# Last gate and mixed low parts shared with GpSimd, second GLA decay two flushes later, gates from slot 0, first pair's keys by halves, three loads by ACT

## Chip, core and metric

The kernel runs on one core of one Trainium2 chip. The metric is the device time of one execution in microseconds (us), median of several runs. Five queues work side by side: TensorE (PE, with its weight loads PEld), VectorE (DVE), ScalarE (ACT), GpSimd (POOL) and SyncE (SP, which only issues transfers). ACT and POOL issue transfers too.

## What is computed

Two layers of a hybrid encoder over 1040 positions (16 meta tokens and 1024 frames) of width 1024, in float32. Cut to what matters here:

```python
xn = rms_norm(h, attn_norm[i])
gq, gk, gv, gr, glr, fq, fk, fv, ff = split(xn @ w_in[i])
log_a = log_sigmoid(glr @ w_alpha_up[i] + b_alpha[i]) / 16
o_gla = rms_norm(gla_chunk_causal(gq / 8, gk, gv, log_a), gla_norm[i]) * silu(gr)   # 4 heads
o_fox = rms_norm(forgetting_attention(fq, fk, fv, log_sigmoid(ff + b_forget[i])), fox_norm[i])  # 8 heads
h = h + concat(o_gla, o_fox) @ w_out[i]
h = h + conv_ffn(rms_norm(h, ffn_norm[i]), w_up[i], conv_w[i], conv_b[i], w_down[i])
# after both layers: rms_norm(h, final_norm)[16:]
```

GLA is linear attention with a decay: per chunk of 64 frames a state S = decay * S + k^T v is kept and read by the queries. FoX is softmax attention with a bias that sums the log of a forget gate.

## The kernel before

Activations lie transposed: eight tiles of 128 features by 1040 positions. A float32 matmul is made of three matmuls in a reduced-width format, `mm3` (L261 to L263): each operand is split into a high part `hi`, a rounded copy made by ACT, and a low part `lo` = x - hi, a subtraction, mostly on DVE. The rounded product hi*hi and the two cross products are added up in PSUM. The helper `split` (L374) does it for activations, at lines L377 (copy by ACT) and L378 (subtraction by DVE); `weights` (L219, L228, L230) does it for weight tiles that SP loads.

A layer has an attention stage and an FFN stage; the change touches the first alone. The attention stage runs in this order.

1. **Head** (`head`). The input tiles are normalised and split in three column chunks (`norm_split`, L341 on ACT and L342 on DVE), and the low-rank and forget projections (L424, L428) and the first GLA projections are made of them. In layer 0 the input comes from memory: `load(0)` in `run` issues eight transfers for the first chunk (L1849), of which those of tiles 1 and 3 go by ACT's queue and six by SP's. Twelve warm-up matmuls (L943) run before.
2. **GLA pair 0 and pair 1.** Each pair has two heads. `gla_products` makes keys, values and queries; when the last key chunk is evacuated, `ev_k` appends `gla_decay` to `self.later`, a list that `flush` empties: it runs what it holds at the end of the next unit of matmuls. `gla_decay` makes z (L507, three PSUM tiles of tag S), a log-sigmoid, a scan over the positions (L510), two more passes and the final product into the keys (L521). `gla_steps` makes the states (L562), reads them (o, L574, which uses three tiles of tag S and one of tag av), normalises each read (L587 to L596) and transposes the result (L603). Between these steps it calls `fill`, which runs the next projection's matmuls in the PE's free time: pair 1's products fill pair 0's steps, and the FoX products of head pair 0 fill pair 1's.
3. **FoX**, `fox`, with four head pairs. A hand-written list of 72 steps, 18 a pair, goes through query tiles; each step is a slot n. In a slot, scores S (L718, L719) go to DVE (L721, bias added, running minimum) and ACT (L733, exp, P); two slots later P is transposed by PE (L754, L747), split (L377, L378) into PT, and in the slot after that used by `av` (L780). `plan(p)` gives the filling work that is spread over the slots from `starts[p]` on: for p = 0 to 2 the products of the next head pair (`fox_products`) and one gate (`gr_products`, silu(gr) times the GLA output), for p = 3 the last gate, for p = 4 the first four tiles of the output projection. `starts` is 4, 22, 40, 58, 62 and 80. At a turn from one plan to the next the old work is drained first.
4. **The turn to the output projection**, slot 62. `plan(4)` splits the mixed activations of the last column chunk (256 columns, seven of the eight tiles, `land[k]` into `mix[k]`, order KORD = 4, 5, 0, 1, 2, 3, 6), asks POOL to load the residual into the tiles just split (L1056), and queues units of matmuls; the other two chunks are split when their first unit begins. Of the last gate, `gr_products(3)`, the result goes straight into `land[3]` (`dst`).

`fox_products` writes keys in two forms, per head: kA holds the high part and kL the low part, each in both halves of the partitions. `ev_k` casts the chunk to kA[0] (L639, ACT), subtracts into kL[0] (L640, POOL), and after the last chunk SP copies halves about, three transfers for kA and three for kL (L644); the third of each overwrites a half that the first two read.

The framework that the kernel is written in orders the instructions of every queue when the program is built, by the order of the code and its own estimates of durations; `high_priority` and the due slots steer it. So an instruction can stand earlier or later in its queue than in the code. Once built, the order in each queue is fixed. In the FFN stage PE's order is that of the code.

Of the kernel before, what the change touches and what calls it, by code (L numbers as in the profile page):

```python
# [170 lines left out]
class Kern:  # L171
# [199 lines left out]
            self.rsqrt_mean(r, ps[:, :n], y0[:, :n], a[:, :n], nm.pop("pin", False))  # L371
        return r

    def split(self, hi, lo, src, scale=None):  # L374
        nc = self.nc
        if scale is None:
            nc.scalar.copy(hi, src)  # L377
            nc.vector.tensor_tensor(out=lo, in0=src, in1=hi.bitcast(F32), op=ALU.subtract)  # L378
        else:
            nc.scalar.mul(hi, src, scale)  # L380
            nc.vector.scalar_tensor_tensor(out=lo, in0=src, scalar=scale, in1=hi.bitcast(F32),
                                           op0=ALU.mult, op1=ALU.subtract)
# [61 lines left out]
    def gla_products(self, lyr, p, gp, pp, nm, g):  # L444
        nc = self.nc
        s = self.slots
        rs = lambda c0, n: self.norm_scale(nm, pp, c0, n)
        g["gk"] = gk = s.get(F32, "gk")
        g["gq"] = gq = s.get(F32, "gq")
        g["gv"] = [s.get(F32, "gv", (128, 8, 128)) for _ in range(2)]  # L450
        g["gvm"] = gvm = gp.tile([64, 2, 128], F32, tag="gvm", name="gvm", bufs=2)
        nc.gpsimd.memset(gvm[:], 0.0)
        if p == 0:
            self.kdm = gp.tile([64, 128], F32, tag="kdm", name="kdm", bufs=1)
            nc.gpsimd.memset(self.kdm[:], 0.0)

        def ev_k(ps, c0, n):
            nc.vector.tensor_tensor(out=gk[:, c0:c0 + n], in0=ps, in1=rs(c0, n), op=ALU.mult)
            if c0 + n == T:
                self.later.append(lambda: self.gla_decay(lyr, p, gp, pp, g))  # L460

        def ev_q(ps, c0, n):
            nc.vector.scalar_tensor_tensor(out=gq[:, c0:c0 + n], in0=ps, scalar=0.125, in1=rs(c0, n),
                                           op0=ALU.mult, op1=ALU.mult)

        def ev_v(hh):
            def ev(ps, c0, n):
                vt = gp.tile([128, 400], F32, tag="vt", name="vt", bufs=3)
                nc.vector.tensor_tensor(out=vt[:, :n], in0=ps, in1=rs(c0, n), op=ALU.mult)
                self.later.append(lambda: self.to_natural(pp, vt, c0, n, self.gv_store(g["gv"][hh], gvm, hh)))  # L470
            return ev
        W = lambda m: self.wm[lyr, m]
        return [(W(M_GK + p), ev_k), (W(M_GV + 2 * p), ev_v(0)), (W(M_GV + 2 * p + 1), ev_v(1)), (W(M_GQ + p), ev_q)]
# [139 lines left out]
    def fox_products(self, lyr, p, work, sp, pp, nm, q, w=None):  # L613
# [21 lines left out]
        def ev_k(ps, c0, n):  # L635
            cs = slice(c0, c0 + n)
            t = sp.tile([128, 400 if self.vt_bufs == 3 else 348], F32, tag="vt", name="kt", bufs=self.vt_bufs)[:, :n]
            nc.vector.tensor_tensor(out=t, in0=ps, in1=rs(c0, n), op=ALU.mult)
            nc.scalar.copy(kA[0][:, cs], t)  # L639
            nc.gpsimd.tensor_tensor(out=kL[0][:, cs], in0=t, in1=kA[0][:, cs].bitcast(F32), op=ALU.subtract)  # L640
            if c0 + n == T:
                for k in (kA, kL):
                    for to, x, own in ((k[1], hi, hi), (k[1], lo, hi), (k[0], hi, lo)):
                        nc.sync.dma_start(to[x, :T].bitcast(F32), k[0][own, :T].bitcast(F32))  # L644
# [25 lines left out]
    def gr_products(self, lyr, h, work, ap, pp, nm, dst=None):  # L670
        nc = self.nc

        def ev(ps, c0, n):
# [8 lines left out]
            nc.scalar.activation(e, e, AF.Exp, scale=-1.0)  # L682
            nc.scalar.activation(y, e, AF.Ln, bias=self.ones[:, 0:1])
            nc.scalar.activation(y, y, AF.Exp, scale=-1.0)
            nc.vector.tensor_tensor(out=og, in0=x, in1=og, op=ALU.mult)
            nc.vector.scalar_tensor_tensor(out=e, in0=e, scalar=1.0, in1=y, op0=ALU.add, op1=ALU.mult)
            nc.vector.scalar_tensor_tensor(out=y, in0=e, scalar=-2.0, in1=y, op0=ALU.add, op1=ALU.mult)
            to = og if dst is None else dst[:, c0:c0 + n]
# [140 lines left out]
    def fox(self, lyr, ap, pp, qs, plan, mix3):  # L829
# [5 lines left out]
        steps = [(p, g, e, ti) for p in range(4) for g in range(5) for e in range(2)  # L835
                 for ti in reversed(range(len(groups[g])))]
        first = [steps.index((p, 0, 0, 1)) for p in range(4)]
        starts = [f + 4 for f in first] + [first[3] + 8, len(steps) + 8]
        cbs, state, due = {}, {}, {}
        work, p_next = plan(-1), 0  # L840

# [7 lines left out]
        for n in range(len(steps) + 8):  # L849
# [30 lines left out]
                    self.fox_mask(cbs[p][e], i - 1)  # L880
                self.fox_schedule(lyr, at, n, p, e, ti, i, tiles, Ps, st, qs[p], ap, pp, mix3)
            parts = [c for c in "12" if (n, "av" + c) in due or (n, "T" + c) in due]
            work.run(fill_us / (1 + len(parts)))
            run(n, "store")
            run(n, "fold")
            for c in parts:
                run(n, "av" + c)
                run(n, "T" + c)
                work.run(fill_us / (1 + len(parts)))
        work.drain()  # L890
        self.slots.put(*cbs[3])
        self.fox_free(qs[3])
# [52 lines left out]
    def attention(self, lyr, nm, hsrc, chunks, feed):  # L945
        tc, nc, s = self.tc, self.nc, self.slots
        self.ch, self.ctiles = CH_HEAD[lyr], CT_HEAD[lyr]
        with tc.tile_pool(name=f"aps{lyr}", bufs=2, space=PSUM, reuse_waits="tile") as pp2, \
# [64 lines left out]
            with tc.tile_pool(name=f"att{lyr}", bufs=2, reuse_waits="tile") as ap, \  # L1013
# [5 lines left out]
                def plan(p):  # L1019
# [15 lines left out]
                    elif p == 4:  # L1035
# [14 lines left out]

                        def split(j):
                            c0, n = chunks[j]
                            for k in KORD:
                                self.split(mix[k][0][:, c0:c0 + n], mix[k][1][:, c0:c0 + n], land[k][:, c0:c0 + n])
                            for m in range(NSPLIT):
                                nc.gpsimd.dma_start(hT[m][:, c0:c0 + n], hsrc[m][:, c0:c0 + n])  # L1056
                        split(2)
# [778 lines left out]
    def run(self):  # L1836
# [3 lines left out]
        def feed(src):  # L1840
# [4 lines left out]
            def load(j):  # L1845
                c0, n = ch[j]
                for k in range(KD):
                    eng = nc.scalar if j == 0 and k in (1, 3) else nc.sync
                    eng.dma_start(land[k][:, c0:c0 + n], self.hT0[k, :, c0:c0 + n])  # L1849
            w = self.narrow_weights(src)  # L1850
            return {"w": w, "load": load,
# [98 lines left out]
```

## Time and profile before

| what | us |
|---|---|
| median of the 3 runs before (lowest to highest) | 2472.36 (2470.87 to 2472.37) |
| the profiled execution: its own time | 2473.53 |
| its span, first to last instruction of the program | 2471.5 |
| outside the span in that execution | 2.0 |
| layer 0: head, GLA, FoX, then FFN | about 0 to 44, 171, 500, then 1240 |
| layer 1: the same | about 1240 to 1286, 1399, 1729, then the end |

A row of the timeline gives start, duration, queue, line, operation, output<-inputs and shape, then in brackets the idle time of the engine before it and who ended that. A row of the waits gives who waited for whom: total us, times, the longest. A row of the windows gives the stretch, its length, then busy time and instructions of each queue, the granted TensorE clock, the busy share of the transfer engines and GB/s. A row on a line or a tile gives shortest, median and longest duration in ns.

### The profile page before, as it was taken

Reading aid. Unit: us, or ns where it says so; the run is one execution under the profiler, and the core shown is the slowest. Engines: PE = TensorE matmul, PEld = TensorE weight load, DVE = VectorE, ACT = ScalarE, POOL = GpSimd, SP = SyncE. Lnnn points to the kernel's source line nnn. Section 1 sums busy time; section 2 is a strip of 40 time slices with the busy share of each in tenths; the row PEclk is TensorE's granted clock in tenths of the full one; section 3 lists DMA queues with packets and bytes.
Section 4 is the critical chain, followed back from the end, with each engine's and each line's share of the span. In section 5 each row is a group of like instructions: output and inputs, shape, how many; then the busy total and the mean of one; then the engine's idle time right before and its main releaser. Section 6 shows DMA issues by size and latency. Waiting matters only on the chain.

```text
span 2471.5 us, 47309 instructions
## 1 busy us (share of the span) xinstructions
PE 2440.1 (99%) x18286; PEld 2358.4 (95%) x18286; DVE 1873.4 (76%) x3769; ACT 1318.1 (53%) x2857; POOL 384.9 (16%) x565
## 2 busy tenths in 40 slices
PE   9999999999999999999999999999999999999998
PEld 8999999999999999999999999999999999998887
DVE  8665776869988888855866666777699888887667
ACT  7345766646555555642543456666465555556433
POOL 2023433210000000100220234331100000001002
PEclk9999999999999999999999999999999999999999
DMA  3222134443322224764312222243433212247722
GB/s 131 74 84 76 43 95 130 126 124 104 119 76 83 83 73 144 185 161 140 118 47 74 80 78 71 71 142 108 146 84 116 91 65 90 82 151 184 210 71 88
DMA packets 121680, 260.39 MB, mean 105 GB/s; under 512 B 15248, under 2 KB 37008, under 8 KB 121456
## 3 DMA queue, kind: packets, MB, share of 16 engines
q1 hardware_dynamic: 97008, 182.18, 23.8%
q0 software_dynamic: 22288, 72.81, 10.5%
q8 instruction: 143, 2.34, 0.4%
q10 hardware_dynamic: 2160, 2.38, 0.3%
q14 instruction: 81, 0.66, 0.1%
HBM read 176.74 MB, written 67.80 MB: 99 GB/s over the span
## 4 chain that ended last, share of the span: by engine, by line
PE 48%; issue 31%; DVE 13%; ACT 4%; DMA 2%; POOL 1%; SPq 0%; DVEq 0%; POOLq 0%; ACTq 0%
PE mm L261 7%; PE mm L263 7%; PE mm L262 7%; PE down L262 4%; PE down L261 4%; PE down L263 4%; PE av L780 3%; PE tr L754 2%; PE S L718 1%; DVE x L1188 1%; DVE S L721 1%; PE S L719 1%; ACT P L733 1%; DVE lo L1163 1%; DMA raw<-in_wm_dram 1%
## 5 line engine op out<-in xcount | busy, mean ns | idle before, releaser
L262 PE MATMUL up<-x,lo 128*128 128x260 f32 x2240 | 632.0, 282 | 0.9 <-DVE lo L1163 0.8
L261 PE MATMUL up<-x,hi 128*128 128x260 f32 x2240 | 632.0, 282 | 0.1
L263 PE MATMUL up<-x,hi 128*128 128x260 f32 x2240 | 632.0, 282 | 0.0
L262 PEld LDWEIGHTS up<-x,lo 128*128 128x128 f32 x2240 | 421.9, 188 | 1.4 <-DVE lo L1163 1.3
L261 PEld LDWEIGHTS up<-x,hi 128*128 128x128 f32 x2240 | 421.9, 188 | 0.4 <-ACT hi L1162 0.3
L263 PEld LDWEIGHTS up<-x,hi 128*128 128x128 f32 x2240 | 422.1, 188 | 0.0
L1162 ACT CAST hi<-raw 128x512 fp32r<-128x512 f32 (+1 forms) x490 | 266.3, 553 | 208.5 <-PE up L263 89.6
L261 PE MATMUL mm<-xh,hi 128*128 128x348 f32 (+6 forms) x1056 | 359.8, 341 | 0.0
L1163 DVE TENSOR_TENSOR lo<-raw,hi 128x512 fp32r<-128x512 f32 (+1 forms) x490 | 286.8, 600 | 81.3 <-ACT hi L1162 80.8
L263 PE MATMUL mm<-xl,hi 128*128 128x348 f32 (+6 forms) x1056 | 339.7, 322 | 0.0
L262 PE MATMUL mm<-xh,lo 128*128 128x348 f32 (+6 forms) x1056 | 338.7, 321 | 0.0
L261 PEld LDWEIGHTS mm<-xh,hi 128*128 128x128 f32 x1056 | 199.5, 189 | 2.3 <-issue 1.4
L262 PEld LDWEIGHTS mm<-xh,lo 128*128 128x128 f32 x1056 | 199.4, 189 | 0.3
L263 PEld LDWEIGHTS mm<-xl,hi 128*128 128x128 f32 x1056 | 198.6, 188 | 0.1
L1144 DVE TENSOR_TENSOR raw<-raw,raw 128x512 f32<-128x512 f32 (+1 forms) x230 | 146.8, 648 | 28.9 <-DMA raw<-in_wd_dram 26.3
L733 ACT ACTIVATE P<-S,m 116x460 f32<-116x460 f32 (+2 forms) x224 | 124.9, 562 | 77.1 <-DVE m L721 74.3
L228 ACT CAST hi<-raw 128x512 fp32r<-128x512 f32 (+2 forms) x152 | 87.4, 576 | 140.5 <-PE mm L263 59.6
L262 PE MATMUL down<-x,lo 128*128 128x260 f32 (+1 forms) x504 | 161.2, 320 | 0.6 <-DVE lo L1163 0.6
L263 PE MATMUL down<-x,hi 128*128 128x260 f32 (+1 forms) x504 | 161.2, 320 | 0.0
L261 PE MATMUL down<-x,hi 128*128 128x260 f32 (+1 forms) x504 | 161.1, 320 | 0.0
L378 DVE TENSOR_TENSOR PT<-tr,PT 116x464 fp32r<-116x464 f32 (+3 forms) x240 | 123.1, 515 | 48.9 <-ACT PT L377 47.2
L1424 POOL DMA_DIRECT2D actd<-cv x44 | 23.6, 535 | 734.5 <-DVE cv L1423 734.5
(313 smaller groups left out, 5957.8 us busy)
## 6 DMA issues: line engine op xcount, KB each, us to landing
raw<-in_wm_dram SPq DMA_DIRECT2D x326, 256.0 KB, 3.0
raw<-in_wd_dram SPq DMA_DIRECT2D x48, 256.0 KB, 4.4
actd<-cv POOLq DMA_DIRECT2D x22, 520.0 KB, 3.0
actd<-cv POOLq DMA_DIRECT2D x22, 512.0 KB, 2.9
cb<-cd SPq DMA_DIRECT2D x16, 520.0 KB, 3.9
kA<-kA SPq DMA_DIRECT2D x24, 260.0 KB, 4.0
kL<-kL SPq DMA_DIRECT2D x24, 260.0 KB, 4.7
st<-actd SPq DMA_DIRECT2D x24, 260.0 KB, 3.7
```

Source lines behind the costliest of these rows:

```text
L228: nc.scalar.copy(hi[:, :n, :], raw[:, :n, :])
L261: nc.tensor.matmul(ps, wh, xh[:, c0:c0 + n], start=first, stop=False, skip_group_check=more)
L262: nc.tensor.matmul(ps, wl, xh[:, c0:c0 + n], start=False, stop=False, skip_group_check=more)
L263: nc.tensor.matmul(ps, wh, xl[:, c0:c0 + n], start=False, stop=last, skip_group_check=more)
L378: nc.vector.tensor_tensor(out=lo, in0=src, in1=hi.bitcast(F32), op=ALU.subtract)
L718: nc.tensor.matmul(S[:rows, :n], q["qA"][e][:, qs], q["kA"][e][:, c0:k1], start=True, stop=False)
L733: nc.scalar.activation(P[:rows, :n], S[:rows, :n], AF.Exp, scale=-1.0, bias=m[:rows, nch - 1:nch], accum_out=(den if nch == 1 else d3[:row ...
L754: nc.tensor.transpose(tr[:w, 3 - j, :rows], P[:rows, o:o + w], id_)
L780: nc.tensor.matmul(av[:, a:b], w.rearrange("p a b -> p (a b)"), x, start=(t == ts[0] and part == 0 and i == 0), stop=(t == last and i == 1))
L1144: nc.vector.tensor_tensor(out=q[out][:, :nk, :], in0=q[a][:, :nk, :], in1=q[b][:, :nk, :], op=op)
L1162: nc.scalar.copy(hi[:, :nk, :], src[:, :nk, :])
L1163: nc.vector.tensor_tensor(out=lo[:, :nk, :], in0=src[:, :nk, :], in1=hi[:, :nk, :].bitcast(F32), op=ALU.subtract)
```

## The change

Seven edits:

- `split` can be told which engine subtracts. In `plan(4)` the subtractions of tiles 5, 1 and 3 (every second one of KORD) go to POOL, in all three chunks; the copies stay with ACT.
- In the last gate alone, the product gx * gog (L685) goes to POOL.
- Pair 1's decay is appended twice more before it runs, so two flushes later. Pair 0's stays.
- `starts[0]` is 0 instead of 4: the filling work of the first head pair is spread over slots 0 to 21.
- In slot 62 the filling work is run at the slot's end, after the slot's store, fold, av and transposes, instead of in two or three shares between them.
- For head pair 0, ACT and POOL write each head's keys from the half where they lie, two instructions of 64 partitions instead of one of 128, and SP copies each half once to the other: four transfers instead of six.
- Of the eight first loads, tile 5's goes by ACT's queue as well.

```diff
-    def split(self, hi, lo, src, scale=None):
+    def split(self, hi, lo, src, scale=None, eng=None):
...
-            nc.vector.tensor_tensor(out=lo, in0=src, in1=hi.bitcast(F32), op=ALU.subtract)
+            (eng or nc.vector).tensor_tensor(out=lo, in0=src, in1=hi.bitcast(F32), op=ALU.subtract)
...
-                self.later.append(lambda: self.gla_decay(lyr, p, gp, pp, g))
+                decay = lambda: self.gla_decay(lyr, p, gp, pp, g)
+                wait = lambda f: lambda: self.later.append(f)
+                self.later.append(wait(wait(decay)) if p else decay)
...
+            if p == 0:
+                for e, own in enumerate((lo, hi)):
+                    nc.scalar.copy(kA[e][own, cs], t[own])
+                    nc.gpsimd.tensor_tensor(out=kL[e][own, cs], in0=t[own], in1=kA[e][own, cs].bitcast(F32),
+                                            op=ALU.subtract)
+                if c0 + n == T:
+                    for k in (kA, kL):
+                        for e, own, oth in ((0, lo, hi), (1, hi, lo)):
+                            nc.sync.dma_start(k[e][oth, :T].bitcast(F32), k[e][own, :T].bitcast(F32))
+                return
...
-            nc.vector.tensor_tensor(out=og, in0=x, in1=og, op=ALU.mult)
+            (nc.vector if dst is None else nc.gpsimd).tensor_tensor(out=og, in0=x, in1=og, op=ALU.mult)
...
-        starts = [f + 4 for f in first] + [first[3] + 8, len(steps) + 8]
+        starts = [0] + [f + 4 for f in first[1:]] + [first[3] + 8, len(steps) + 8]
...
-            work.run(fill_us / (1 + len(parts)))
+            turn = n == starts[4]
+            if not turn:
+                work.run(fill_us / (1 + len(parts)))
...
-                work.run(fill_us / (1 + len(parts)))
+                if not turn:
+                    work.run(fill_us / (1 + len(parts)))
+            if turn:
+                work.run(fill_us)
...
-                            for k in KORD:
-                                self.split(mix[k][0][:, c0:c0 + n], mix[k][1][:, c0:c0 + n], land[k][:, c0:c0 + n])
+                            for i, k in enumerate(KORD):
+                                self.split(mix[k][0][:, c0:c0 + n], mix[k][1][:, c0:c0 + n], land[k][:, c0:c0 + n],
+                                           eng=nc.gpsimd if i % 2 else None)
...
-                    eng = nc.scalar if j == 0 and k in (1, 3) else nc.sync
+                    eng = nc.scalar if j == 0 and k in (1, 3, 5) else nc.sync
```

## The prediction

> **What bounds the kernel now.** I began with the page: its first two lines of numbers, then the waits of PE, then the windows around the places that the change touches.
>
> ```profile
> span 2471.5 us, 47309 instructions
> PE 2440.1 (99%) x18286; PEld 2358.4 (95%) x18286; DVE 1873.4 (76%) x3769; ACT 1318.1 (53%) x2857; POOL 384.9 (16%) x565
> ```
>
> PE is busy 2440.1 of 2471.5 us, so all idle time of PE is 31.4 us, and the change removes no matmul. It can win only from those 31.4 us, and from matmuls that run at a low clock. Which of them it can reach, the waits of PE tell (total, times, longest):
>
> ```profile
> PE mm L263 <- DVE ml L378: 3.5, 2, 1.8
> PE tr L754 <- DVE PT L378: 3.1, 4, 1.2
> PE S L718 <- ACT P L733: 1.9, 4, 0.6
> ...
> PE av L780 <- DVE PT L378: 1.4, 5, 0.4
> PE tr L603 <- DVE on L596: 1.4, 1, 1.4
> PE z L507 <- DVE on L596: 1.4, 1, 1.4
> PE mm L428 <- DVE xl L342: 1.3, 1, 1.3
> ...
> PE av L780 <- ACT PT L377: 0.7, 2, 0.3
> ...
> PE o L574 <- DVE B L390: 0.4, 1, 0.4
> ```
>
> Nearly all of them come once a layer, at four places: the turn to the output projection (ml, PT), the start of FoX (P), the second decay (on, B) and, in layer 0 only, the head (xl). The two turns are the worst:
>
> ```profile
> 445.00:465.00 20.00, 16.61 (x128) 15.77 (x127) 19.87 (x58) 17.28 (x49) 6.22 (x12) 1.00 0.37 105
> 1673.00:1693.00 20.00, 16.88 (x129) 15.56 (x127) 19.87 (x59) 17.63 (x50) 6.03 (x12) 1.00 0.34 98
> ```
>
> In 20 us PE is idle 3.4 and 3.1, while DVE is busy 19.87: there DVE is the bound, and POOL, at 6, is free.
>
> **The turn.** These are the last two steps of DVE ahead of PE's first wait in layer 0, then PE's two long waits and what stands between them:
>
> ```profile
> 450.90 0.51 DVE L685 TENSOR_TENSOR gog<-gx,gog 128x344 f32<-128x344 f32 x1
> 451.33 1.09 DVE L378 TENSOR_TENSOR ml<-h,mh 128x256 fp32r<-128x256 f32 x3
> ...
> 451.80 0.39 PE L263 MATMUL mm<-ml,hi 128*128 128x256 f32 x1 [1.76 <-DVE ml L378]
> ...
> 453.09 0.79 PE L780 MATMUL av<-PT,V 116*128 116x232 f32 x6
> 453.71 0.49 PE L754 MATMUL tr<-ident,P 116*116 116x116 f32 x3
> ...
> 457.62 0.61 PE L754 MATMUL tr<-ident,P 116*116 116x116 f32 x4 [1.22 <-DVE PT L378]
> ```
>
> The first fill of the slot needs, 1.76 us before 451.80, a low part that DVE begins at 451.33. Three edits act here. The gate product (0.51) leaves DVE ahead of that low part. Three of the seven subtractions leave DVE: 3 x 0.42 = 1.3 us for this chunk (the row of three takes 1.09, since they overlap a little; 0.42 is one alone). And the slot's av and transposes, 453.09 to 454.20, so 1.1 us of PE work that came behind the stall, now come before the fill.
>
> On POOL such a subtraction is dearer; the same shape stands there in other places, as do two instructions that show a conflict:
>
> ```profile
> L355 POOL TENSOR_TENSOR r<-r,sq 128x256 f32<-128x256 f32 x14 | 10.6, 760 | 7.1 <-ACT sq L354 6.9
> ...
> 153.62 0.92 POOL L640 TENSOR_TENSOR kL<-kt,kA 128x344 fp32r<-128x344 f32 x1 [1.69 <-issue]
> ...
> 153.66 0.90 DVE L315 TENSOR_TENSOR oa<-oa,ovv 128x4 f32<-128x4 f32 x1
> ...
> 154.86 0.16 DVE L315 TENSOR_TENSOR oa<-oa,ovv 128x4 f32<-128x4 f32 x1
> ```
>
> 0.76 us on POOL for 0.42 on DVE. And a DVE operation on 4 columns, 0.16 us by itself, took 0.90 when it began 0.04 us behind a POOL subtraction, and ended 0.02 behind it: it was held until POOL was done. The remaining DVE subtractions read two SBUF operands like it. The worst price per chunk is therefore 3 x 0.76 = 2.3 held less 1.3 saved = 1.0 us lost on DVE; the best is 1.3 won. I take half of the loss, 0.5, since ACT's copies come in between and DVE has PSUM-sourced work for some of that time.
>
> The Trainium skill's page "SBUF — State Buffer", section "SBUF: two separate sides", speaks against this edit: DVE operations with two SBUF inputs and GpSimd share a port pair as an exclusive lock, held for a whole instruction, and the loser blocks. The row of 0.90 agrees. By that rule alone the sharing costs the 1.0 and not the 0.5.
>
> Per turn: the first stall, 1.76, loses 1.1 (PE work ahead) and 0.5 (gate product) and gets back 0.5 (held DVE), a gain of 1.1. The second, 1.22 and 1.07, is a PT subtraction late on the same full DVE queue; by then DVE has lost a second 0.5 or three 0.42s, and I take half, 0.6. Of the small ones behind (0.4 and 0.2) I take 0.2. That is 1.9 a turn, **3.8** for both layers; ends: 6.5 won (all idle time of both windows), 2.0 lost.
>
> **The start of FoX.** The four waits for P and two for PT are 1.9 + 0.7 = 2.6 us, about 183 to 191 in layer 0 and 1410 to 1418 in layer 1. The keys come late:
>
> ```profile
> 159.67 1.17 SPq L644 DMA_DIRECT2D kA<-kA  x2
> 160.88 2.28 SPq L644 DMA_DIRECT2D kL<-kL  x2
> ...
> 166.93 0.46 SPq L644 DMA_DIRECT2D kL<-kL  x1
> ...
> kL<-kL SPq DMA_DIRECT2D x24, 260.0 KB, 4.7
> ```
>
> SP cannot issue the third copy of kL until the first two have been read and landed, and this last issue, at 166.93, lands 4.7 us later by the median, about 171.6; scores that need kL cannot run before. By halves nothing is overwritten: the four transfers go out at about 160 to 162.5 and the last lands near 167, some 4.5 us earlier. The edit adds, a layer, three ACT casts and three POOL subtractions:
>
> ```profile
> L639 ACT CAST kA<-kt x24: 478/482/486, 153.0 to 1616.9; 128x348 fp32r<-128x348 f32 x16, 128x344 fp32r<-128x344 f32 x8
> ...
> L640 POOL TENSOR_TENSOR kL<-kt,kA x24: 917/928/953, 153.6 to 1618.3; 128x348 fp32r<-128x348 f32 x16, 128x344 fp32r<-128x344 f32 x8
> ```
>
> The length along the columns is the same, so 0.48 and 0.93 each. ACT and POOL have idle time at 150 to 165 (POOL's wait of 1.69 above); only the last chunk's pair, 1.4 us, delays the transfers, which is in the 162.5. If that cover were gone, the price is 1.4 us a layer out of 4.5.
>
> `starts[0]` = 0 spreads the same fill over 22 slots instead of 18, so each gets 18/22 of it, but slots 0 to 3 now have some in their own order. PE stays fed while the first P are made. What is late next are the slots from 4 on, with 18% less fill each; the PT waits in the first pairs are 0.1 to 0.2 us, and I put 0.7 us on that and the added ACT and POOL work, for both layers. I take **2.2** of 2.6 as won; ends: 2.6 won, 0.8 lost.
>
> **The decay.** Pair 1's decay runs between pair 0's reads and their norms:
>
> ```profile
> 92.11 2.32 DVE L510 TENSOR_TENSOR_SCAN A<-reset,B 128x1040 f32<-128x1040 bf16 x1
> ...
> 97.11 0.23 PE L603 MATMUL tr<-ident,on 16*128 16x16 f32 x1 [1.38 <-DVE on L596]
> 97.12 1.22 DVE L521 TENSOR_TENSOR gk<-gk,B 128x1040 f32<-128x1040 f32 x1
> ...
> 115.06 0.71 PE L603 MATMUL tr<-ident,on 128*128 128x128 f32 x5
> ...
> 128.58 1.04 PE L536 MATMUL tr<-ident,gk 128*128 128x128 f32 x8
> ```
>
> The scan alone holds DVE 2.32 us while PE waits 1.38 for a norm, and the z tiles hold PSUM that the reads want (0.4, the wait of o for B). In layer 1 PE stands at z itself, 1.4 us, since its PSUM tile is still being read by a norm. Two flushes are two units of matmuls, some 7 us: z moves behind the first norms. All of it is 1.4 + 1.4 + 0.4 = 3.2 us. What is late next: the third z takes the PSUM tile that the last norm reads, and the decay's 8 us of DVE meet the last norms, whose transposes stand at 115.06. The decay ends with its product into the keys, 98.3 before; two units and the wait for the third z bring it to about 114, and the keys are transposed at 128.58, so that end keeps a cover of 14 us. I take **2.0** won; ends: 3.2 won, 1.4 lost (one such wait more).
>
> **The head.** ACT's queue is free until 3.6:
>
> ```profile
> 1.19 3.24 SPq L1849 DMA_DIRECT2D hin<-in_hT_dram  x6
> 3.62 0.71 ACT L244 CAST both<-raw 128x256 fp32r<-128x256 f32 x2 [1.59 <-DMA raw<-in_wr_dram]
> ...
> 8.74 0.52 ACT L341 ACTIVATE xh<-hin,gain 128x272 fp32r<-128x272 f32 x1 [1.08 <-DMA hin<-in_hT_dram]
> ...
> 0.00:16.00 16.00, 13.25 (x70) 11.57 (x71) 10.47 (x25) 12.34 (x27) 3.47 (x15) 0.89 0.89 296
> ```
>
> An issue takes 0.54 on SP, so the last input goes out 0.5 earlier. The transfer engines are 0.89 busy over these 16 us, and behind these inputs come the first weights, for which PE waits next. So **0.5** of the 1.3 idle. The granted clock of this row, 0.89, is 0.11 x 16 = 1.8 us lost: PE runs at half clock for a stretch of some 3.5 us, behind the idle time. Ends: 3.1 won (idle and clock), 1.8 lost (a second such stretch).
>
> **Sum.** -3.8 - 2.2 - 2.0 - 0.5 + 0.7 = -7.8 us. The profiled execution would have a span of 2463.7 and take 2465.7; it was 1.2 above the median, so against the median of 2472.4 the forecast is **2464.6**, 0.3% faster. A measurement here tells about 0.2%, 4.9 us.
>
> **Rivals.**
>
> 1. The held subtractions decide the turn: DVE's stand until POOL's are done, as in the row of 0.90, and PT and S wait behind them in DVE's queue. For it: that row, and DVE at 19.87 of 20 us. Against: PE's order at the turn changes too. The turns win nothing and lose 0.5 each: 2472.4 - 4.7 + 0.7 + 1.0 = 2469.4. Chance 0.20. This is the case that the Trainium skill's "SBUF — State Buffer", named above, would give.
> 2. The edits do not do what they say, because the queues' orders are set at build time and the order in the code is only one input. For it: in this row a matmul of the fill stands in PE's queue right behind the first slot's scores, four slots before the code asks for it,
>
> ```profile
> 172.96 0.38 PE L261 MATMUL mm<-xh,hi 128*128 128x344 f32 x1
> ```
>
> so slot 0 instead of 4 may change nothing there, and a displaced decay may only move its wait. FoX and decay win nothing: 2472.4 - 3.8 - 0.5 + 0.7 = 2468.8. Chance 0.14.
> 3. The half-clock stretch goes as well. Less idle time in the stretch before it would be the cause. The forecast less 1.8: 2462.8. Chance 0.08. The Trainium skill's "TensorE: Matmul & The Clock Gate", Part 1, has the gate decided by activity in free-running windows of about 3.4 us; the stretch of some 3.5 us agrees, and by that page the phase varies from run to run.
> 4. Slower: POOL is in order, and its residual loads wait for the splits:
>
> ```profile
> 452.96 1.09 POOL L1056 DMA_DIRECT2D h<-in_hT_dram  x2 [5.36 <-DVE fa L315]
> ```
>
> POOL stood 5.36 us before this load, harmless now. If a subtraction that PE needs, or the last gate's product, stands behind such a load in POOL's queue, PE waits up to 5.4 us at each turn, as soon as the load's wait is longer than the 1.1 us of PE work ahead of the fill. Turns: 10.8 less 2 x 1.1 = 8.6 lost, the rest as forecast: 2472.4 + 8.6 - 4.0 = 2477.0; with the 1.0 of rival 1, 2478.0. Against: POOL has 14 of 20 us free, and the loads come behind the subtractions in the code. Chance 0.10.
>
> **How the numbers follow.** The forecast has 0.48, and its own range is 2461 to 2468. Of it 0.42 lies below 2467.5 and 0.06 in the middle; rival 3 is faster; of rivals 1 and 2 a quarter (0.08) is faster, the rest the same; of rival 4, 0.08 is slower and 0.02 the same. Faster 0.58, same 0.34, slower 0.08. The range for 8 in 10 leaves out rival 4 and the fast tail of the forecast and of rival 3: 2460 to 2473.
>
> **What would show it.** In the changed kernel's waits of PE, `mm L263 <- DVE ml` should fall from 3.5 to about 1.3, `S L718 <- ACT P` below 0.4, and `tr L603` and `z L507 <- DVE on` together from 2.8 to about 1. Scores that read kL should begin about 167 instead of 172. If DVE subtractions of the turn show 0.7 us or more beside POOL's, rival 1 holds; if PE waits at the turn for POOL ml, rival 4. The prediction is wrong if PE's idle time moves to new places: it should be about 24 us, from 31.4.

## The result, and the profile after

| | us |
|---|---|
| before, on the same chip (5 runs, lowest to highest) | 2472.36 (2470.64 to 2474.08) |
| after (5 runs, lowest to highest) | 2481.79 (2479.55 to 2483.69) |
| after : before | 1.0036, interval 1.0025 to 1.0047 |
| forecast | 2464.6 (2460 to 2473) |

The changed kernel is 9.4 us **slower**. The forecast had it 7.8 us faster, and its range ends 8.8 us below the measured time. The lines of the changed kernel have moved down: L718 is now L730, L754 is L766, L780 is L792, and `split` is still L377 and L378.

The page's first lines of the changed kernel:

```profile
span 2481.4 us, 47324 instructions
...
PE 2445.4 (99%) x18286; PEld 2362.7 (95%) x18286; DVE 1889.3 (76%) x3745; ACT 1322.0 (53%) x2863; POOL 415.4 (17%) x595
```

PE's idle time is 2481.4 - 2445.4 = 36.0 us; it was 31.4, and 24 was forecast. DVE has 24 instructions fewer and is 15.9 us busier (6.8 of these stand in e4 too, below, whose turn is as before): that is the first sign that its instructions became longer. The waits of PE of the changed kernel (who waited for whom, total us, times, longest):

```profile
PE av L792 <- DVE PT L378: 7.5, 6, 3.4
PE tr L766 <- DVE PT L378: 6.9, 7, 2.8
PE S L730 <- ACT P L745: 2.9, 4, 1.3
PE ssq L366 <- DVE r L355: 2.8, 3, 1.0
```

What the change aimed at is gone: mm no longer waits for ml (3.5 before), tr and z no longer for on (2.8), mm L428 no longer for xl (1.3). In their place PE waits 14.4 us for the transposed probabilities PT that DVE subtracts, against 3.1 + 1.4 = 4.5 before. PE waits nowhere for POOL. The two turns, in the view of the windows (stretch, length, busy time and instructions of PE, PEld, DVE, ACT, POOL, then PE's granted clock):

```profile
441.00:461.00 20.00, 14.08 (x79) 13.17 (x78) 20.00 (x44) 13.94 (x40) 12.45 (x19) 0.77 0.36 106
448.50:455.30 6.80, 6.37 (x32) 6.10 (x31) 6.80 (x19) 4.83 (x14) 2.77 (x5) 0.50 0.44 129
1674.00:1694.00 20.00, 13.62 (x84) 12.66 (x83) 20.00 (x44) 13.68 (x40) 12.30 (x18) 0.83 0.35 105
```

In the 20 us of layer 0's turn DVE gets through 44 instructions, where before it did 58 in an equally full window, and PE through 79 instead of 128. So DVE has handed work over and does less in the same time. The middle row shows a second novelty: for 6.8 us PE has half its clock.

The timeline says why DVE is slower. DVE's queue of the changed kernel at layer 0's turn (start, duration, queue, line, operation, tiles, shape):

```profile
442.34 1.13 DVE L378 TENSOR_TENSOR ml<-h,mh 128x400 fp32r<-128x400 f32 x1
...
443.78 1.69 DVE L698 SCALAR_TENSOR_TENSOR ge<-ge,gy 128x348 f32<-128x348 f32 x1
...
446.39 0.63 DVE L378 TENSOR_TENSOR PT<-tr,PT 116x464 fp32r<-116x464 f32 x1
...
447.54 1.95 DVE L701 SCALAR_TENSOR_TENSOR h<-gy,gog 128x348 f32<-128x348 f32 x1
...
450.86 0.95 DVE L693 TENSOR_SCALAR ge<-gx 128x344 f32<-128x344 f32 x1
...
454.89 1.54 DVE L820 TENSOR_TENSOR fon<-ff,fy 116x128 f32<-116x128 f32 x2
456.35 1.31 DVE L699 SCALAR_TENSOR_TENSOR gy<-ge,gy 128x344 f32<-128x344 f32 x1
...
458.27 1.05 DVE L378 TENSOR_TENSOR PT<-tr,PT 116x464 fp32r<-116x464 f32 x2
```

and POOL's queue in the same stretch:

```profile
442.28 0.75 POOL L378 TENSOR_TENSOR ml<-h,mh 128x256 fp32r<-128x256 f32 x1
...
444.07 1.01 POOL L378 TENSOR_TENSOR ml<-h,mh 128x384 fp32r<-128x384 f32 x1
...
447.68 1.43 POOL L378 TENSOR_TENSOR ml<-h,mh 128x256 fp32r<-128x256 f32 x2
...
450.70 0.91 POOL L697 TENSOR_TENSOR gog<-gx,gog 128x344 f32<-128x344 f32 x1 [0.74 <-DVE gx L690]
...
455.22 2.07 POOL L378 TENSOR_TENSOR ml<-h,mh 128x384 fp32r<-128x384 f32 x2
```

L698 lasts from 443.78 to 445.47, POOL's 384-column subtraction from 444.07 to 445.08. L701 begins at 447.54, POOL's two subtractions end at 449.11, and L701 at 449.49. Each ends about 0.4 us behind POOL, nearly its own length: it was held until POOL was done. L820 and L699 lengthen in the same way beside POOL's next two subtractions, at 455.22. Two rows over the whole run give the usual durations (shortest, median, longest in ns, by line):

```profile
L701 DVE SCALAR_TENSOR_TENSOR h<-gy,gog x6: 497/514/1947, 435.4 to 1690.9; 128x348 f32<-128x348 f32 x4, 128x344 f32<-128x344 f32 x1, 128x336 f32<-128x336 f32 x1
...
L378 DVE TENSOR_TENSOR PT<-tr,PT x240: 259/627/645, 176.8 to 1728.9; 116x464 fp32r<-116x464 f32 x80, 116x116 fp32r<-116x116 f32 x16, 116x348 fp32r<-116x348 f32 x16, 112x112 fp32r<-112x112 f32 x8
```

L701, with two SBUF operands, takes 0.51 as a rule and 1.95 here. The subtraction into PT, which has one operand in PSUM, is never longer than 0.645 in 240 executions, whatever POOL does. It isn't slow; it stands in order behind the slow ones, at 446.39 and, in the next slot, at 458.27, and PE waits (start, duration, queue, and in brackets the idle time before):

```profile
447.07 0.85 PE L792 MATMUL av<-PT,V 116*128 116x256 f32 x5 [3.08 <-DVE PT L378]
...
458.95 1.03 PE L766 MATMUL tr<-ident,P 116*116 116x116 f32 x4 [2.41 <-DVE PT L378]
```

### The profile page after: what moved, and what is told of

It reads as the page before. It is cut to its first block, busy times and chain, and to the rows that moved or that the text cites. A ratio compares the mean times of both kernels' runs of the same rounds, so it can differ in the third digit from the quotient of the medians.

```text
span 2481.4 us, 47324 instructions
## 1 busy us (share of the span) xinstructions
PE 2445.4 (99%) x18286; PEld 2362.7 (95%) x18286; DVE 1889.3 (76%) x3745; ACT 1322.0 (53%) x2863; POOL 415.4 (17%) x595
## 3 DMA queue, kind: packets, MB, share of 16 engines
q0 software_dynamic: 22288, 72.81, 10.5%
## 4 chain that ended last, share of the span: by engine, by line
PE 49%; issue 31%; DVE 13%; DMA 3%; ACT 3%; POOL 1%; SPq 0%; DVEq 0%; POOLq 0%; ACTq 0%
PE mm L261 8%; PE mm L263 7%; PE mm L262 7%; PE down L261 4%; PE down L262 4%; PE down L263 4%; PE av L792 3%; PE tr L766 2%; PE S L730 1%; DVE S L733 1%; DMA raw<-in_wm_dram 1%; PE S L731 1%; PE wo L263 1%; PE wo L261 1%; PE wo L262 1%
## 5 line engine op out<-in xcount | busy, mean ns | idle before, releaser
L378 DVE TENSOR_TENSOR PT<-tr,PT 116x464 fp32r<-116x464 f32 (+3 forms) x240 | 122.7, 515 | 48.9 <-ACT PT L377 47.8
```

The lines of the kernel that those rows point to most:

```text
L378: (eng or nc.vector).tensor_tensor(out=lo, in0=src, in1=hi.bitcast(F32), op=ALU.subtract)
```

## The experiments

All are the changed kernel with edits undone, the kernel before with one or two edits alone, or one of these with something added. "Before" on the three chips was 2473.03, 2472.66 and 2473.17. By the intervals, a difference between two of these rows is uncertain by some 2 us: one of 3 us is just told from nothing, one of 0.5 or 1.6 isn't.

| kernel | us | to before | interval |
|---|---|---|---|
| e3: low parts and gate product on DVE, rest as changed | 2467.03 | 0.9977 | 0.9966 to 0.9988 |
| e4: e3 with the slot's old order too | 2466.48 | 0.9972 | 0.9963 to 0.9982 |
| e1: low parts on DVE, gate product on POOL | 2470.21 | 0.9988 | 0.9979 to 0.9998 |
| e2: gate product on DVE, low parts shared | 2476.13 | 1.0014 | 1.0005 to 1.0024 |
| g2: as e2, one low part of seven on POOL | 2470.13 | 0.9990 | 0.9981 to 0.9999 |
| g1: as e3, with idle subtractions on POOL | 2469.80 | 0.9987 | 0.9978 to 0.9995 |
| e7: before, with shared low parts alone | 2483.75 | 1.0046 | 1.0033 to 1.0060 |
| f1: changed kernel with filling matmuls | 2484.41 | 1.0045 | 1.0032 to 1.0057 |
| e9: before, with the displaced decay alone | 2468.06 | 0.9979 | 0.9970 to 0.9988 |
| e8: before, with slot 0 and keys by halves | 2472.43 | 0.9997 | 0.9988 to 1.0005 |
| keys: before, with keys by halves alone | 2473.32 | 1.0003 | 0.9994 to 1.0012 |
| b1: e4 with FoX's fill from slot 4 again | 2468.10 | 0.9981 | 0.9972 to 0.9990 |

### Which part of the turn costs: e1 to e4

The four kernels undo the edits of the turn, one by one and together:

```diff
# e1, e3, e4
-                                           eng=nc.gpsimd if i % 2 else None)
+                                           eng=None)
# e2, e3, e4
-            (nc.vector if dst is None else nc.gpsimd).tensor_tensor(out=og, in0=x, in1=og, op=ALU.mult)
+            nc.vector.tensor_tensor(out=og, in0=x, in1=og, op=ALU.mult)
# e4
-            turn = n == starts[4]
+            turn = False
```

> The changed kernel with all low parts of the mix made by DVE again; the gate product stays on GpSimd and the slot's order stays changed. Theory 'held' (DVE stands still until GpSimd's subtractions are done, PT comes late, PE's idle time there halves its clock): about 2468, 10 to 14 below the changed kernel's 2481.8, and no half-clock stretch at the two turns. Theory 'product' (the gate product on GpSimd does it): 2478 or more. Theory 'order' (the fill put at the end of slot 62 leaves PE without work): 2476 or more, with the wait of av for PT still near 3 us.

> The changed kernel with the last gate's product on DVE again; the low parts stay shared, the order stays changed. Theory 'held': 2479 to 2482, the waits for PT near 3 us and the half-clock stretches stay. Theory 'product': about 2468. Theory 'order': 2479 to 2482.

> The changed kernel with low parts and product on DVE; only the order of slot 62 stays changed at the turn. Theory 'held': 2465 to 2468, as the run with the low parts back or 1 to 2 lower. Theory 'order': 2474 or more. If product and subtractions have to be on DVE together to undo the loss, this run is fast and the two single ones are not.

> The whole turn as before: decay, slot 0, keys and loads alone are changed. By the two traces the stages ahead of the turns win 4.0 us in layer 0 and 2.6 in layer 1, so all theories of the turn say about 2466 (0.3% below before). A theory that the loss comes from the other edits (a later phase of transfers, other tiles in other places) says 2472 or more.

With all three undone the kernel is 6.5 us faster than before. The order of the slot is worth nothing that can be told: e3 - e4 = 0.5 us. The gate product on POOL costs 2470.21 - 2467.03 = 3.2 us, and 5.7 where the low parts are shared as well (after - e2). The shared low parts cost 2476.13 - 2467.03 = 9.1, and 11.6 where the gate product is on POOL too (after - e1). Together 14.8 us, more than the whole loss. Theory 'held' has e1, e3 and e4 right; e2 lies below its 2479 to 2482, since the gate product has a part that the theory gave to the low parts alone.

The same DVE queue in e2 and e3 can be added up. First e3, which has neither on POOL:

```profile
439.76 0.51 DVE L697 TENSOR_TENSOR gog<-gx,gog 128x348 f32<-128x348 f32 x1
...
443.25 0.51 DVE L699 SCALAR_TENSOR_TENSOR gy<-ge,gy 128x348 f32<-128x348 f32 x1
...
448.00 0.15 DVE L314 SCALAR_TENSOR_TENSOR fa<-fy 116x4 f32<-116x4 f32 x1
...
449.50 0.48 DVE L820 TENSOR_TENSOR fon<-ff,fy 116x128 f32<-116x128 f32 x2
...
452.60 1.06 DVE L378 TENSOR_TENSOR PT<-tr,PT 116x464 fp32r<-116x464 f32 x2
...
462.16 0.57 DVE L378 TENSOR_TENSOR ml<-h,mh 128x400 fp32r<-128x400 f32 x1
```

and e2, with the shared low parts:

```profile
439.70 0.51 DVE L697 TENSOR_TENSOR gog<-gx,gog 128x348 f32<-128x348 f32 x1
...
441.49 1.92 DVE L378 TENSOR_TENSOR ml<-h,mh 128x400 fp32r<-128x400 f32 x1
...
444.70 0.88 DVE L699 SCALAR_TENSOR_TENSOR gy<-ge,gy 128x348 f32<-128x348 f32 x1
...
450.34 0.99 DVE L314 SCALAR_TENSOR_TENSOR fa<-fy 116x4 f32<-116x4 f32 x1
...
452.99 1.51 DVE L820 TENSOR_TENSOR fon<-ff,fy 116x128 f32<-116x128 f32 x2
...
455.53 1.05 DVE L378 TENSOR_TENSOR PT<-tr,PT 116x464 fp32r<-116x464 f32 x2
```

and the subtractions of e2's POOL beside which the first, third and fourth of these rows lengthen (441.49, 450.34 and 452.99):

```profile
441.95 1.02 POOL L378 TENSOR_TENSOR ml<-h,mh 128x384 fp32r<-128x384 f32 x1
...
450.08 1.23 POOL L378 TENSOR_TENSOR ml<-h,mh 128x384 fp32r<-128x384 f32 x1 [2.55 <-ACT mh L377]
...
453.31 1.04 POOL L378 TENSOR_TENSOR ml<-h,mh 128x384 fp32r<-128x384 f32 x1
```

From the gate product to the PT on which PE waits longest, e3 takes 452.60 - 439.76 = 12.84 us, e2 15.83: 2.99 more. The held instructions make up (1.92 - 0.57) + (0.88 - 0.51) + (0.99 - 0.15) + (1.51 - 0.48) = 3.6. Against that stand three 256-column subtractions fewer, which follow one another every 0.34 us here, so 1.0, and one 400-column subtraction more, 0.5: it belongs to a later chunk, but the order set at build time has drawn it forward into this stretch. 3.6 - 1.0 + 0.5 = 3.1, which is the 2.99. So the sum of the held instructions is the delay of this PT, and not one of the four is among the subtractions of the chunk that is being split: a later chunk's low part, a gate step and two steps of FoX's norm are. And POOL's side of it is mostly the other chunks' work as well: 1.35 + 0.84 + 1.03 = 3.2 of the 3.6 us stand beside the three 384-column subtractions above. The 2.99 isn't the whole of e2's loss, which is 9.1 us in two layers; the rest is found with f1, below.

### How the cost grows: g2, and the shared part on the old base: e7

```diff
# g2, on e2
-                                           eng=nc.gpsimd if i % 2 else None)
+                                           eng=nc.gpsimd if i == 3 else None)
```

> Gate product on DVE; of the seven low parts of a chunk one (the fourth) on GpSimd in place of three. Measured so far: none 2467.0, three 2476.1. Theory held, each GpSimd subtraction holding DVE for about its own length: a third of the cost, 2469 to 2471. Rival: one is the dose at which the saving of 0.42 and the hold balance, since DVE has PT and S from PSUM to do meanwhile: 2466 to 2468. Rival: the cost lies in the first subtraction on the path and not in their number: 2474 to 2476.

One low part in place of three costs 2470.13 - 2467.03 = 3.1 us, a third of 9.1. With one and three as the two points, the cost goes with the number of POOL's instructions; there is no first, free one.

e7 undoes every other edit of the changed kernel.

> The kernel before with the shared low parts alone, the slot's order and all else as before. Prediction's step: 0.5 lost on DVE a chunk, 1.0 at most, so 2473 to 2475. Theory held: the cost is that of the step from none to three on the other base, 9.1 us: 2480 to 2483. Rival: part of the 9.1 belongs to the changed order of the turn's slot, in which av and the transposes stand behind PT directly and not behind the fill; then 2475 to 2479.

2483.75 - 2473.17 = 10.6 us, at least as much as on the other base and just above the range expected. The cost doesn't need the changed order of the slot.

### Held, or waiting for POOL's results: g1

The kernel e3, where POOL makes three subtractions per chunk that nothing needs:

```diff
+                                if i % 2:
+                                    w1 = min(n, 304)
+                                    x = ap.tile([128, 304], BF16, tag="scr", name="scr", bufs=1)[:, :w1]
+                                    nc.gpsimd.tensor_tensor(out=x, in0=land[k][:, c0:c0 + w1],
+                                                            in1=mix[k][0][:, c0:c0 + w1].bitcast(F32), op=ALU.subtract)
```

> The kernel with low parts and gate product on DVE again (2467.0 measured), where GpSimd in addition makes three of each chunk's seven subtractions a second time into a scratch tile that nothing reads (for the two wide chunks the first 304 columns of 384 or 400). DVE, ACT and PE have the same work and depend on none of it. Theory held: DVE's operations on two SBUF operands take 1 us and more where they meet one of these, PT comes late, and the time rises to that of the shared low parts (2476) or above it, up to 2484, since DVE keeps its own subtractions too. Rival: the shared low parts cost time because PE or a load waits for the part that GpSimd makes (0.74 us instead of 0.42); then extra work that nobody waits for costs nothing: 2466 to 2468.

The time rises by 2.8 us (2469.80 - 2467.03). Both expectations miss: idle work on POOL isn't free, but it costs less than a third of the sharing. The rows of g1's DVE and POOL tell why:

```profile
440.23 0.52 DVE L697 TENSOR_TENSOR gog<-gx,gog 128x348 f32<-128x348 f32 x1
...
446.39 0.42 DVE L815 TENSOR_REDUCE fv<-fon 116x4 f32<-116x256 f32 x1
446.73 0.83 DVE L693 TENSOR_SCALAR ge<-gx 128x344 f32<-128x344 f32 x1
447.47 0.70 DVE L816 TENSOR_TENSOR fv<-fv,fd 116x4 f32<-116x4 f32 x1
...
454.22 1.06 DVE L378 TENSOR_TENSOR PT<-tr,PT 116x464 fp32r<-116x464 f32 x2
```

```profile
445.81 2.35 POOL L1076 TENSOR_TENSOR scr<-h,mh 128x256 bf16<-128x256 f32 x3 [2.06 <-ACT mh L377]
...
451.12 4.51 POOL L1076 TENSOR_TENSOR scr<-h,mh 128x304 bf16<-128x304 f32 x3
...
455.98 0.83 POOL L1076 TENSOR_TENSOR scr<-h,mh 128x304 bf16<-128x304 f32 x1
```

The first three run until 448.16. While they begin, DVE reads PSUM, or sums up one SBUF tile (L815), and isn't held; then L693 and L816 lose 0.5 each (0.33 and 0.16 in e3). The next three take 4.51 us where 3 x 0.83 = 2.5 would do: here POOL was held, by 2.0 us, and DVE ran on. In these rows the engine that was there first ran on and the other was held (in three rows of other kernels the records have it otherwise, see the last section). From the gate product to the same PT it is 454.22 - 440.23 = 13.99 us, so DVE loses 1.15 in g1, and 2.99 in e2. So the hold needs no dependence between the two engines, but its price is a matter of what stands beside POOL's instructions, and of the rest of the queue's order; g1 has other neighbours than e2, and its 2.8 us don't price the 9.1. That the shared kernels also wait for POOL's results is not seen: no row of PE's waits in the changed kernel names POOL.

### Does the half clock cost anything: f1

Twelve matmuls of ones in front of the late av products keep PE busy while it would stand; DVE and POOL keep their instructions:

```diff
+            if n == starts[4]:
+                ps = pp.tile([128, 512], F32, tag="mm", name="fillmm")
+                for _ in range(12):
+                    nc.tensor.matmul(ps[:, :128], self.ones[:], self.ones[:], start=True, stop=True)
             for kind in ('av0', 'T0'):
                 run(n, kind)
```

> The changed kernel with 12 extra matmuls of ones (128x128, about 0.24 us each, 2.8 us in all) in PE's queue directly ahead of the late av products of the turn's slot, so that PE works while it would stand 3.08 and 3.37 us for PT; DVE and POOL are as in the changed kernel, so PT comes as late as before. Theory A: the half-clock stretches of 6.83 us at 448.5 and 1680.7 (and 3.41 at 458.7) come from PE's idle time and cost PE half their length, 3.4 + 3.4 + 1.7. With the fillers they go: the time falls by 6 to 8 us from 2481.8 to about 2475, the clock reads 0.999, the PT waits that begin at 443.99 shrink below 0.7, wo starts at about 509 in layer 0. Theory B: what PE loses is the time in which DVE is late; a slow PE hides behind it, and the clock costs nothing: 2480 to 2482, with the idle time turned into more waits at 452 to 460. Theory C: the fillers themselves delay the chain: 2483 or more.

The window that had half the clock, in f1:

```profile
448.50:455.30 6.80, 4.69 (x36) 3.97 (x34) 6.80 (x18) 5.18 (x14) 3.41 (x5) 1.00 0.42 134
```

The clock is 1.00 there, the matmuls run at their usual speed, and the time is 2484.41: not lower, and as a number where theory C has it. PE only arrives sooner at the next PT:

```profile
458.93 0.61 PE L766 MATMUL tr<-ident,P 116*116 116x116 f32 x4 [4.08 <-DVE PT L378]
```

In the changed kernel this wait was 2.41 and ended at 458.95. The same PT comes at the same time; what the slow clock took, the wait gave back. So the fillers delay nothing here, and theory B holds for this stretch. Why f1 is 2.6 us above the changed kernel was not tried; its traces have half the clock at 460.1 and, new, at 1692.3, both behind longer waits for PT (4.08 and 4.04).

Kernels without any fillers agree. b1 has half the clock for 3.41 us from 448.3, e4 doesn't, and both run the same 82 matmuls from the end of the wait for ml (446.99 and 447.42) to a later av product (459.10 and 459.53): 12.11 us in each. e4's wait of 1.20 for PT in between is what b1 doesn't have.

A stretch that no wait follows is paid, however. The half clock of e2 begins at the end of its long wait for PT, and PE doesn't stand again in this turn. The waits of e3 and e2, and the window in e2:

```profile
453.29 0.61 PE L766 MATMUL tr<-ident,P 116*116 116x116 f32 x4 [1.35 <-DVE PT L378]
```

```profile
456.22 0.68 PE L766 MATMUL tr<-ident,P 116*116 116x116 f32 x4 [3.85 <-DVE PT L378]
```

```profile
456.70:460.10 3.40, 3.40 (x19) 3.40 (x18) 3.40 (x7) 3.23 (x10) 2.35 (x3) 0.51 0.02 6
```

From there to the next scores e3 takes 3.0 us (to 456.26) and e2 5.0 (to 461.24). e2 has four fill matmuls more in between, 0.12 us each at full clock; the other 1.6 us are the clock. With the 2.99 of the late PT, and less a wait of 0.41 that e3 still has behind it (459.58), e2's layer 0 loses 4.2 us. Layer 1 has the same pair of wait and stretch (3.69, then half the clock from 1685.4). Twice 4.2 is 8.4, of the 9.1 measured. So the hold makes PT late, and the clock adds to it where PE goes straight on: about a third of e2's price. In the changed kernel only layer 0 has such a stretch, from 458.7; f1 doesn't remove it.

### The edits that win or don't: e9, e8, keys, b1

e9, e8 and the kernel with the keys alone undo all edits but those named; b1 undoes, beside e4's, this one:

```diff
-        starts = [0] + [f + 4 for f in first[1:]] + [first[3] + 8, len(steps) + 8]
+        starts = [f + 4 for f in first] + [first[3] + 8, len(steps) + 8]
```

> The kernel before with the second pair's decay two flushes later, alone. The prediction's step: tr and z no longer wait 1.38 and 1.36 for on, o not 0.4 for B: 2.0 won of 3.2, 2470.4. Theory A: the whole 3.2 goes, 2469. Theory B: the waits move to the third z or to the last norms and nothing is won: 2472. No wait of S for P above 0.7 near 263, if that one belongs to the fill.

> The kernel before with two edits alone: FoX's fill spread from slot 0, and the first pair's keys written by halves. The prediction's step: 2.2 us won of the 2.6 of S and PT waits at 183 to 191 and 1410 to 1418, so 2470.2; the first score that reads kL falls from 171.2 to about 167. Theory A (the two looks with the turn undone): these waits go, but a new wait of S for P of 1.2 to 1.3 us a layer stands at about 263 and 1490, where less fill is left, so a net 0 to 1: 2471 to 2473. Theory B: the new wait is another edit's (the displaced decay), and 2470 holds without it.

> The kernel before with the first pair's keys written by halves, alone. The prediction has the keys' late landing hold the first scores, with up to 2.6 us to win at 183 to 191 and 1410 to 1418. Theory from the traces so far: PE is never idle between 96 and 186, the first scores stand behind the fill in its queue, and keys that land earlier free nothing: 2471 to 2474, with S's waits for P still 1.9 to 2.2 in four. Rival: with the keys early and the fill late, PE comes to the P sooner and these waits go: 2469 to 2470.

> The changed kernel with low parts, gate product and order of the turn as before, and the fill of FoX's first pair from slot 4 again as before; left are the displaced decay, the keys by halves and the third load by ACT. If the 1.3 and 1.2 us that S waits for P at 263 and 1487 come from the fill being spread over 22 slots, they go here: 2466.5 less up to 2.5, so 2464 to 2466. If the spread fill is what fed PE at 183 to 191, then S and PT waits of up to 2.6 come back there and the time stays at 2466.5 or rises to 2467.5.

The displaced decay wins 4.6 us by itself (interval 3.0 to 7.4): theory A, the whole 3.2 and perhaps a little more. No wait of tr, z or o for on or B above 0.2 us is left in e9. The last product of the decay, and the transpose of the keys that follows, are these rows of DVE and PE in e9:

```profile
108.62 1.24 DVE L523 TENSOR_TENSOR gk<-gk,B 128x1040 f32<-128x1040 f32 x1 [0.67 <-ACT B L522]
```

```profile
124.04 1.04 PE L538 MATMUL tr<-ident,gk 128*128 128x128 f32 x8
```

The keys by halves win nothing (1.0003), and with slot 0 nothing either (0.9997). In e8 S's waits for P grew, from 1.9 to

```profile
PE S L730 <- ACT P L745: 2.8, 4, 1.2
```

The waits of PE for P near 183 to 191 are gone, and new ones of 1.18 each stand at 264.7 and 1492.5, in the first pair's later slots, which have less fill now. They stand in every kernel that has slot 0, and in none of e9, b1 and the kernel with the keys alone. What the fill's spread gave at one end it took at the other. b1 doesn't contradict it: without slot 0 2468.10, against 2466.48 in e4, a difference that one measurement can't tell here (and a little more than the 2466.5 to 2467.5 expected at most); and as b1 is the decay, the keys and the third load by ACT, and has the time of the decay alone (2468.06), the keys and the load together win nothing.

**The fastest version** is e4, the changed kernel without the three edits of the turn: 2466.48, 0.9972 of before and 15.3 us below the changed kernel.

## Why the prediction was wrong, step by step

**The turn, -3.8 (the runs: 14.8 + 0.5 lost): off by 19 us, and the step that failed.** The prediction bounded the sharing at 1.0 us lost, "3 x 0.76 = 2.3 held less 1.3 saved", took 0.5, entered it once a turn, and booked the gate product as 0.5 won a turn. The bound was none, for three reasons.

- It counts POOL's three 256-column subtractions of the chunk that slot 62 splits. The other two chunks' go to POOL as well, wider ones, and the order set at build time puts some ahead of the PT that PE waits for: in e2's layer 0 they make 3.2 of 3.6 us held. What they hold are mostly not DVE's subtractions, of which alone the prediction spoke: gate steps (0.51 becomes 1.69 and 1.95 in the changed kernel), a later chunk's low part (0.57 becomes 1.92 in e2) and even instructions on four columns (0.15 becomes 0.99).
- The gate product, moved to POOL, is one more holder (L693 at 450.86, 0.95 for 0.34), and this hold is a term that the sum put at nothing: not 1.0 won in both layers but 3.2 to 5.7 lost.
- The longer waits bring half the clock, which the sum has in the head alone: 1.6 us in e2's layer 0.

And the second stall, 1.22, was to lose 0.6 with DVE's lighter queue; it grew to 2.41, as each held microsecond comes on top of the same full queue. The window before had said it: with DVE busy 19.87 of 20 us, there was no idle time for a hold to fall into.

**Rival 1** named this mechanism and priced it at 2469.4, a turn 0.5 worse than nothing. The mechanism is right; the size was off: 1.0 for both turns, where the runs show 15.3. The Trainium skill's page "SBUF — State Buffer", section "SBUF: two separate sides", has the lock go to whichever began first, for the whole instruction, and the other blocked. The traces agree that one engine stands until the other is done: DVE is held by 1.4 us at 447.54 in the changed kernel, and POOL by 2.0 us at 451.12 in g1. That the first to begin goes first they don't show: by the records L701 began 0.14 us before POOL's subtraction, and was the one held.

**PE's work ahead of the fill, 1.1 a turn: nothing.** In the changed kernel the av products came forward, but waited for a PT from the same DVE queue (3.08 at 447.07). In e3, where they don't, the waits for ml fell from 3.5 to about 1.0 (0.52 and 0.50), and weights' low parts (wl, 1.1 in two) came in exchange; e3 - e4 is 0.5, so the time shows no gain.

**FoX's start, -2.2: -0.2.** The prediction took the late landing of kL for the cause of the waits at 183 to 191. But these are waits for P, and in the kernel before PE has no wait above 0.3 us between 98 and 186: nobody waited for the keys there. That was to be read from the waits of PE, which name no DMA. In one execution, e7's, which has the old keys, the first score with kL did wait for the transfer (its row of PE's timeline):

```profile
171.77 0.64 PE L731 MATMUL S<-kL,qA 128*116 128x460 f32 x2 [1.05 <-DMA kL<-kL]
```

Over the runs the keys alone are worth nothing that can be told. The 0.7 put on the spread fill was the other half of the error: the new waits are 1.3 + 1.2 = 2.5, as much as the old ones.

**The decay, -2.0: the way right, the size too small.** It gave 4.6 with an interval of 3.0 to 7.4; the best end, 3.2, lies in it, the 2.0 taken doesn't, and why it's more than the waits come to stays open. One reading was off: the scan doesn't hold DVE while PE waits. By the prediction's rows it ended at 94.43, and PE stood from 95.73 on, behind the rest of the decay on DVE. Its cover held too: the product into the keys stands at 108.6 in e9, not at 114, and the keys are transposed at 124.0, 14 us after its end.

**The head, -0.5: nothing that can be told apart.** Rival 3's half-clock stretch is gone in the changed kernel, but not by the load: of two kernels that leave the loads as they were, e8 and the one with the keys alone, the first 16 us read (same columns as the windows above)

```profile
0.00:16.00 16.00, 14.02 (x88) 13.54 (x89) 11.06 (x26) 12.83 (x29) 3.48 (x15) 1.00 0.91 302
```

```profile
0.00:16.00 16.00, 13.65 (x72) 12.03 (x73) 10.59 (x26) 12.45 (x28) 3.48 (x15) 0.89 0.90 302
```

and e9 reads 1.00 as well. So it comes and goes with the loads unchanged.

**Rival 2**, orders set at build time, was half right: FoX won nothing, for another reason, while the same build-time order brought later chunks' low parts forward, DVE's and POOL's, into the worst place. **Rival 4** had the right sign by the wrong mechanism: no row of PE's waits names POOL.

**Sum by what was measured:** low parts and gate product +14.8, order +0.5, decay -4.6, start -0.2, loads 0: +10.5, for +9.4 measured.

## What to carry to other kernels

Before giving GpSimd work on SBUF, look at what VectorE runs in those microseconds: if it is the bound there and its instructions read SBUF alone, price the move at a hold of up to a whole GpSimd instruction for every GpSimd instruction that stands beside them, short ones included, and not at the work that is handed over. Count all the GpSimd instructions that the edit makes, and not those of one place. A queue that is 99% busy in the stage has no cover, whatever its average over the span. And a transfer that lands late is worth moving only if a wait of the bounding engine names it.

## What the runs showed of the hardware

- A VectorE instruction of 0.15 us on four columns took 0.99 beside a GpSimd subtraction, one of 0.51 took 1.95 across two; one with a PSUM operand never lengthened in 240 executions. A `TENSOR_SCALAR` with a single SBUF input (L693) was held as well: 0.34 became 0.95.
- GpSimd is held as well: three subtractions of 0.83 took 4.51 us.
- The held instructions on 348 or 400 columns end 0.38 to 0.44 us behind POOL's, so they do nearly all their work after it (those on four columns end 0.01 or 0.02 behind), though by the records three of them began 0.14 to 0.46 before it (441.49 in e2, 443.78 and 447.54 in the changed kernel). In all three cases POOL was issuing transfers when they began. Whether an issue holds DVE, or POOL's subtraction holds it ahead of its recorded begin, is open; in e3 DVE's subtractions at 448.49 and 448.89 keep their usual 0.42 and 0.68 beside two issues.
- PE's clock fell to half for 3.41 or 6.83 us, once or twice the same length, with idle times of 2.4 to 3.4 us just before or at its begin in the changed kernel, and of 1.75 to 1.77 in e8, b1 and the kernel with the keys alone, but not behind the 1.75 of e4 nor the 1.76 of before and e9. The Trainium skill's "TensorE: Matmul & The Clock Gate", Part 1, has free-running windows of about 3.4 us, which agrees with both lengths. Half the clock of a PE that waits for another engine anyway cost nothing: with it and without it the same PT ended the wait, at 458.95 and 458.93, and the same 82 matmuls took 12.11 us. Where no wait followed it cost 1.6 us of a stretch of 3.41 (e2).
